# An attention stage issued from a table of work pieces, with queries scaled ahead of their turn

## The chip, the cores and the metric

The kernel runs on one core of a Trainium2 chip. The core has a matrix engine (PE, whose weight loads are listed apart as PEld), three engines for elementwise work (DVE, ACT, POOL), a queue engine (SP) that issues the DMAs, and two on-chip memories: SBUF, which all engines reach, and PSUM, into which PE writes its results. The metric is the device time of one execution in microseconds (us); lower is better.

## The reference

One layer of a hybrid network is computed for 128 context tokens and 512 latent tokens (640 columns in all), in float32. Cut to what matters here:

```python
u = rms_norm(h, g_pre1) * (1 + scale1) + shift1
q, k, v, b_gate, c_gate, x_in, g_att, g_conv = split(u @ w_in)
q = rms_norm(q.reshape(B, N, 16, 64), q_norm)      # 16 query heads, 4 key heads of 64
k = rms_norm(k.reshape(B, N, 4, 64), k_norm)
# latent tokens: rotary on q and k, keys and values = cached context + own
p = softmax(q @ k.T * 64 ** -0.5)                  # one softmax over 640 keys (context: 128)
A = (p @ v) @ w_att_out
Bm = (b_gate * dwconv3(c_gate * x_in)) @ w_conv_out
m = sigmoid(g_att) * A + sigmoid(g_conv) * Bm
h = h + gate1 * rms_norm(m @ w_o, g_post1)
# then the feed-forward part with w_up, dwconv3, silu, w_down and its own norms
```

The modulation vectors (scale, shift, gate) come from `silu(c) @ w_ada + b_ada`.

## The kernel before

Every matmul with weights or activations is done as three products of a high and a low part: a tensor is copied by ACT into a rounded high part (`hi`) and the rest is formed by a subtraction into a low part (`lo`). `mm3` (lines 161 to 163) issues the three products. Cutting a weight tile of 128 x 1024 in this way is one ACT copy and one subtraction (`cut_hi`, lines 700 and 701; `split`, lines 135 and 136, in the later stages).

The attention stage (from line 514 on) runs over four groups `g`, one for each key head with its four query heads. A group has nine steps. Step 0 is the context's own attention (128 queries, 128 keys, four heads). Steps 1 to 8 (class `Step`, `n` from 0 to 7) each take one tile of 128 latent queries and two of its four heads `h`, against 640 keys. A step consists of:

- scores: 12 matmuls (L603) into two rooms of PSUM (`ps2`, two banks each; there are three such rooms). Queries `QH`, `QL` are raw rotated queries; the factor of their normalisation, `rq`, is not in them yet.
- `exps(h)`: the negative maximum on DVE (L739), that maximum times `rq` on ACT (L741), the exponential on ACT with `scale=rq` and the sum of each row (L742).
- `shares()`: the reciprocal of the sums on DVE (L745) and for each `h` the product of 128 x 640 with it on POOL (L750). The tiles `pr` have two buffers.
- `turned()`: DVE turns both halves in blocks of 32 x 32 into the tile `PT` (L755).

Between the steps stand pieces of other work:

- a query tile: `q_part` (24 matmuls into one of two single PSUM banks `S1`), `q_rotate` (rotary: three products on DVE, L543 and L545, their sum on POOL, L546), `squares` on ACT (L550), `factors` on DVE and POOL (L556 to L558), and later `q_turn`: two transposes on PE (L584) into a single bank, the high part on ACT (L587), the low part on DVE (L590).
- the modulation of the second half (`ada2_mm`, 32 matmuls at L214 from two raw tiles of `w_ada`, and `ada2_keep`, one sum on DVE, L235), sixteen times in all; at the end `ada2_fold`.
- nine cuts of raw weight tiles (units 10 to 18) and, in the last two groups, the two gate columns of 128 (`gate_part`, weights of units 16 and 17).
- the product with the values (class `Values`) for each half of the eight steps: `own` (context, L773) and `part` (L782), into one room `ps2` and both single banks `S1`; then `sums` (ACT copies the odd halves to SBUF, L798 and L799; DVE adds the even ones, L805 and L808), `high` on ACT (L812) and `low` (L816, POOL). `part` is called in two goes of five pairs, or of three and seven.

What sets the order: PE, ACT and DVE (and SP outside) execute in the order in which the program issues to them; this is a hand-written order (`manual_schedule`). POOL's instructions in this stage are placed by the compiler's scheduler. The loop over `i` from 0 to 8 has one fixed pattern for each `i`, with small tables (`turn`, `qt`, `room`, `CUTS`, `BLK`): scores of step `i`; a query's turn; a modulation piece; a part of the values; both `exps`; the low part of the turned query; `turned` of the step before; a query part; the factors of the query before; `sums` and `high` of the values if they are complete; `shares`; `low`; a cut; rotary and squares of the query part. Behind the last group come gate 1 (columns 256 to 640), the fold, `turned` of the last step, the change to the sigmoid table (L978), the last values in three pieces, and their sums.

The raw tiles (weights and `w_ada`) come through a ring of three buffers on SP's queue; the list `ring` holds their order, and `ring_used` asks for the next ones when a piece has been used.

## Time and profile before

| | |
|---|---|
| median of 3 runs | 1163.02 us (1162.43 to 1163.92) |
| profiled execution | 1161.01 us, its span in the profile 1159.2 us |
| mean granted clock of PE | 0.968 |
| busy, share of the span | PE 1105.9 us (95%), DVE 827.6 (71%), ACT 564.6 (49%), POOL 173.2 (15%) |
| first score matmul of step 1 in group 0 | at 77.5 us |
| step 0 of groups 1, 2, 3 | at 126.3, 180.6, 235.1 us |
| step 8 of group 3; first matmul behind the stage | at 278.6 us; at 306.7 us |

Times in the profile are counted from the start of the span. A line such as "L750 POOL TENSOR_TENSOR pr<-pr,sm 128x640" is one line of the program on one engine, with the tile that it writes and those that it reads. Busy time counts an engine as busy while an instruction runs on it; PE's matmuls are pipelined, so that a busy PE need not be at its peak. The granted clock is the share of its full speed that PE was allowed. A view of the waits says for each engine on which instruction it waited and which instruction released it; the chain of work is followed back from the last instruction of the kernel to what released each step.

### The profile page before, as it was taken

Reading aid. Unit: us, or ns where it says so; the run is one execution under the profiler, and the core shown is the slowest. Engines: PE = TensorE matmul, PEld = TensorE weight load, DVE = VectorE, ACT = ScalarE, POOL = GpSimd, SP = SyncE. Lnnn points to the kernel's source line nnn. Section 1 sums busy time; section 2 is a strip of 40 time slices with the busy share of each in tenths; the row PEclk is TensorE's granted clock in tenths of the full one; section 3 lists DMA queues with packets and bytes.
Section 4 is the critical chain, followed back from the end, with each engine's and each line's share of the span. In section 5 each row is a group of like instructions: output and inputs, shape, how many; then the busy total and the mean of one; then the engine's idle time right before and its main releaser. Section 6 shows DMA issues by size and latency. Waiting matters only on the chain.

```text
span 1159.2 us, 21001 instructions
## 1 busy us (share of the span) xinstructions
PE 1105.9 (95%) x8605; PEld 1019.1 (88%) x8605; DVE 827.6 (71%) x1235; ACT 564.6 (49%) x1007; POOL 173.2 (15%) x205
## 2 busy tenths in 40 slices
PE   8988788888899999999999999999999999999997
PEld 6787677777799999999999988999999999998786
DVE  5578777766454788888745447888888888888644
ACT  4366555556233544554542246565454555555431
POOL 2057566665000000000000012000000000002001
PEclk9998897988899999999999999999999999999999
DMA  9665335333022322323332543333332333315632
GB/s 336 200 173 149 104 97 134 92 93 92 23 71 60 104 74 87 96 73 92 91 110 74 180 150 130 108 114 105 112 101 91 96 115 103 114 60 182 222 110 90
DMA packets 188989, 133.47 MB, mean 115 GB/s; under 512 B 16914, under 2 KB 171086, under 8 KB 188878
## 3 DMA queue, kind: packets, MB, share of 16 engines
q1 hardware_dynamic: 188782, 132.11, 37.2%
q8 instruction: 67, 1.10, 0.4%
q14 instruction: 28, 0.23, 0.1%
q10 hardware_dynamic: 112, 0.04, 0.0%
HBM read 120.01 MB, written 12.24 MB: 114 GB/s over the span
## 4 chain that ended last, share of the span: by engine, by line
PE 84%; DVE 6%; ACT 3%; POOL 3%; issue 2%; DMA 1%; DVEq 0%; POOLq 0%; SPq 0%; ACTq 0%
PE b L1029 44%; PE b L161 9%; PE b L163 9%; PE b L162 9%; POOL pr L750 3%; PE s1a L161 2%; PE s1a L162 2%; PE s1a L163 2%; PE s L603 2%; ACT pr L742 1%; DVE Y L1513 1%; DVE PT L755 1%; PE s L161 1%; PE s L163 1%; DVE mx L739 1%
## 5 line engine op out<-in xcount | busy, mean ns | idle before, releaser
L1029 PE MATMUL b<-ZB,whi 128*128 128x322 f32 x1024 | 228.5, 310 | 0.0
L1029 PEld LDWEIGHTS b<-ZB,whi 128*128 128x128 f32 x1024 | 173.8, 189 | 1.6
L1029 PE MATMUL b<-ZB,wlo 128*128 128x322 f32 x512 | 159.4, 311 | 0.0
L1029 PE MATMUL b<-MT,whi 128*128 128x320 f32 x608 | 134.1, 308 | 0.0
L1029 PEld LDWEIGHTS b<-MT,whi 128*128 128x128 f32 x608 | 101.6, 188 | 0.0
L1029 PEld LDWEIGHTS b<-ZB,wlo 128*128 128x128 f32 x512 | 96.2, 188 | 0.0
L750 POOL TENSOR_TENSOR pr<-pr,sm 128x640 f32<-128x640 f32 x64 | 86.7, 1377 | 47.5 <-DVE sm L745 46.7
L1029 PE MATMUL b<-MT,wlo 128*128 128x320 f32 x304 | 93.8, 308 | 0.0
L1513 DVE SCALAR_TENSOR_TENSOR Y<-C,cffn,Y 128x642 f32<-128x642 f32 x88 | 80.9, 921 | 0.9
L1016 ACT ACTIVATE whi<-SUM 128x1024 fp32r<-128x1024 f32 x40 | 42.2, 1055 | 79.6 <-DVE SUM L1483 77.2
L136 DVE TENSOR_TENSOR wlo<-raw,whi 128x1024 fp32r<-128x1024 f32 (+1 forms) x31 | 33.7, 1086 | 52.5 <-ACT whi L135 52.0
L1029 PE MATMUL b<-UH,whi 128*128 128x320 f32 x228 | 70.5, 309 | 0.0
L1029 PE MATMUL b<-UL,whi 128*128 128x320 f32 x228 | 70.4, 309 | 0.0
L1029 PE MATMUL b<-UH,wlo 128*128 128x320 f32 x228 | 70.2, 308 | 0.0
L1020 DVE TENSOR_TENSOR wlo<-raw,whi 128x1024 fp32r<-128x1024 f32 (+1 forms) x51 | 50.4, 1020 | 25.3 <-ACT whi L1016 24.4
L1016 ACT ACTIVATE whi<-WB 128x1024 fp32r<-128x1024 f32 x38 | 40.1, 1055 | 54.8 <-DVE WB L1124 54.8
L1037 ACT ACTIVATE p<-b 128x322 f32<-128x322 f32 (+1 forms) x78 | 34.3, 440 | 58.2 <-PE b L1029 58.2
L603 PE MATMUL s<-KH,Q 64*128 64x320 f32 x256 | 44.5, 343 | 18.2 <-ACT pr L742 17.6
L742 ACT ACTIVATE pr<-s,mr,rq 128x640 f32<-128x640 f32 x64 | 56.7, 885 | 4.1 <-ACT mr L741 0.4
L1029 PEld LDWEIGHTS b<-MT,wlo 128*128 128x128 f32 x304 | 57.0, 188 | 0.0
L1040 DVE TENSOR_TENSOR C<-b,p 128x322 f32<-128x322 f32 x40 | 19.7, 492 | 52.3 <-PE b L1029 51.8
L603 PEld LDWEIGHTS s<-KH,Q 64*128 64x128 f32 x256 | 29.8, 191 | 29.5 <-ACT pr L742 24.3
(382 smaller groups left out, 3166.3 us busy)
## 6 DMA issues: line engine op xcount, KB each, us to landing
raw<-in_w_in_dram SPq DMA_DIRECT2D x48, 512.0 KB, 3.5
RAW<-in_w_up_dram SPq DMA_DIRECT2D x40, 512.0 KB, 5.4
raw<-in_w_ada_dram SPq DMA_DIRECT2D x32, 512.0 KB, 4.8
raw<-in_w_down_dram SPq DMA_DIRECT2D x22, 512.0 KB, 4.0
actd<-Y SPq DMA_DIRECT2D x18, 321.0 KB, 2.8
AFB<-actd SPq DMA_DIRECT2D x18, 321.0 KB, 4.5
XT<-in_w_ada_dram SPq DMA_DIRECT2D x9, 512.0 KB, 5.8
raw<-in_w_conv_out_dram SPq DMA_DIRECT2D x9, 512.0 KB, 3.7
```

What stands on the lines that cost most here:

```text
L136: eng.tensor_tensor(out=lo[:, :n], in0=raw, in1=hi[:, :n].bitcast(F32), op=ALU.subtract)
L161: PE.matmul(out, ah, bh, start=start, stop=False)
L162: PE.matmul(out, ah, bl, start=False, stop=False)
L163: PE.matmul(out, al, bh, start=False, stop=stop)
L603: PE.matmul(outs[h], q[rows, pi, :], kk[rows, g, ks], start=n == 0, stop=n == 2, tile_position=(64 * h, 0))
L742: S.activation(self.pr[:, h, :], self.sc[h], AF.Exp, bias=low, scale=rs, accum_out=self.sm[:, h:h + 1])
L750: G.tensor_tensor(out=self.pr[:, h, :], in0=self.pr[:, h, :], in1=self.sm[:, h:h + 1].broadcast_to((128, NTOK)), op=ALU.mult)
L1016: S.activation(to[0], raw, AF.Copy)
L1020: V.tensor_tensor(out=lo, in0=raw, in1=hi.bitcast(F32), op=ALU.subtract)
L1029: PE.matmul(out, p[:, ws], q[:, k, :], start=start and k == 0 and n == 0, stop=stop and k == 3 and n == 2, skip_group_check=True)
L1037: S.activation(t, pair[j][b], AF.Copy)
L1513: V.scalar_tensor_tensor(out=y, in0=crows(j)[i][:, d:d + NACT], scalar=cffn[:, 44 * d + o:44 * d + o + 1], in1=y, op0=ALU.mult, op1=ALU.add)
```

## The change

A table `PLAN` of four texts, one for each group, takes the place of the loop's fixed pattern. Each word is one piece of work; the pieces are issued to all engines in the order of the words. The letters: S scores, x exponentials of one half, r reciprocal, m shares of one half (on POOL with P, on ACT with A), t turn of the shares; Q query part (numbers from 5 on are the next group's tiles), R the rotary products, p their sum (POOL, or DVE with V), q squares, F factors, T query turn, l its low part; A modulation matmuls, K their sum; c a cut (low part on POOL with P, on DVE with V); V values, u one of three ACT copies, a one of three sums, H high, L and M low; G, g, J gate parts; f fold; w the warm-up of the sigmoid; v a load of values. The letters a and b choose a single bank.

What the pieces do differently:

- POOL's instructions of this stage are issued in the written order too.
- Queries are multiplied by their factors `rq` on POOL (`q_scale`, 128 x 256) before they are turned, from tile 3 of group 0 on. The exponential then has no scale, and the small ACT product of the maximum is gone for these tiles; the context's maximum needs no product in groups 1 to 3.
- Of the shares, some halves are done by ACT (a copy with a scale), the others by POOL.
- The low part of a cut is done on POOL or DVE, as the table says.
- The values of a half are one piece of ten pairs instead of two pieces; copies, sums, high and low are pieces of their own, and the sums over the room of two banks are two instructions instead of four.
- Modulation matmuls always go to the last 128 columns of a single bank instead of a room `ps2` at times; queries' buffers `qf` are three instead of two.
- The gate columns are computed in blocks of 320 columns (before 256, 256 and 128, and 256 and 384), gate 1 whole at the end in eight pieces. The warm-up of the sigmoid stands in step 2 of group 3.
- The ring of raw tiles follows the order of A and c in the table. The same loads are made.

```diff
--- before
+++ after
+PLAN = (
+    """
+    cV
+    S1 R3 Q4a cP x00 x10 r0 q3 x11 q4 R4 m00 p3P t0
+    S2 Q5b r1 m11A x20 m10P p4P x21 F3 t1 Aa R5 r2 F4 K
+    S3 q5 m20A m21A T3b x30 Q6a x31 p5V q6 F5 l3 t2 T4b R6 r3
+    S4 l4 m31A m30P x40 x41 p6P t3 Q7a R7 r4 q7 m40P
+    S5 m41A T5b x50 x51 Aa l5 K cP t4
+    S6 r5 m51A F6 x60 m50A V0 x61 p7P t5 u00
+    S7 F7 u10 u20 a00 r6 x71 Q9a x70 a20 a10 m61A r7 m60P q9 R9 t6 T7b H0
+    S8 l7 p9P m71A m70A Aa x80 F9 K x81 t7 Q8b r8 m81P T6a R8 q8 m80A p8P l6 L0P
+    """,
+    """
+    S0 T4b x00 Aa t9 K l4
+    S1 x10 r0 x11 r1 m00 F3 m10P t0 V1 cV u01 u11
+    S2 u21 a01 a11 T3a x21 m11P x20 Q5b a21 t1 R5 r2 q5 l3 m20A p5P
+    S3 m21P x30 Q6b F5 x31 q6 t2 r3
+    S4 H1 Aa R6 m30A x41 m31P p6P Q7b L1P x40 F6 t3 K T5a
+    S5 q7 r4 R7 l5 m40P m41A T6b x50 Aa x51 K p7P l6 cP t4
+    S6 r5 V0 m50A m51A x60 x61 t5 r6 u00 m61P F7
+    S7 u10 u20 a00 m60P a10 x71 Q9a x70 a20 Ab t6 H0 r7 m71A R9 q9
+    S8 m70A K x80 L0P p9P F9 x81 Q8b t7 r8 m81P R8 q8 p8P T7a m80A l7
+    """,
+    """
+    S0 T4b x00 t9
+    S1 x10 x11 Aa K l4 r0 r1 m00 F3 t0
+    S2 cP m11A V1 m10A x20 x21 u11 t1 r2 a11
+    S3 u01 u21 m20P m21P a01 cP T3b x30 a21 Q5a v x31 t2
+    S4 q5 R5 Q6a l3 r3 m30A x40 p5P x41 m31P Ab F5 q6 t3 r4 R6
+    S5 p6P H1 L1P m41A m40A K F6 T5b x50 x51 t4 l5 Q7a q7
+    S6 R7 T6b r5 m51P Aa x61 l6 p7P m50A K F7 x60 r6 V0 t5 m61P u10 u00
+    S7 a10 Ab u20 m60P a00 x70 x71 a20 H0 Q8a q8 t6 r7
+    S8 K m71A m70P R8 Q9b x81 x80 t7 p8P R9 T7a r8 q9 L0P l7 m81P p9P F9 m80A
+    """,
+    """
+    S0 x00 t9
+    S1 Ab x10 r0 x11 m00 G1a K T4b g1 F3 l4 r1 t0 m10P
+    S2 m11P x20 x21 t1 V1 w
+    S3 r2 u01 a01 u21 Aa u11 x30 m21A a21 m20P x31 a11 t2 r3
+    S4 G0b m30A x40 m31P x41 t3 r4 g0
+    S5 m41A K T3a m40P x50 Ab x51 l3 K t4 r5 H1
+    S6 x61 m51P V0 L1V m50P x60 cP r6 u00 u20 t5 m60A a00
+    S7 x70 m61P Aa a20 u10 x71 t6 r7 m70A
+    S8 x80 J0 x81 J1 m71P K t7 r8 m81P J2 cP fa J3 m80A t8 J4 J5 J6 a10 V2 J7 u12 u02 u22 a12 a02 H0 L0V a22 H2 M2
+    """,
+)
...
+        def rotate_sum(t, out, tm, eng=G):
+            if t:
+                eng.tensor_tensor(out=out, in0=out, in1=tm, op=ALU.add)
...
-        def q_rotate(pz, g, t, eng=G):
-            tm = at.tile([128, 4, HD], F32, tag="z", name=nm("zt"), bufs=ZB)
-            qf = qfs[g, t] = at.tile([128, 4, HD], F32, tag="qf", name=nm("qf"), bufs=2)
-            rotate(pz, t, 0, qf, tm, eng)
+        def q_mults(pz, g, t):
+            tm = at.tile([128, 4, HD], F32, tag="z", name=nm("zt"), bufs=ZB) if t else None
+            qf = qfs[g, t] = at.tile([128, 4, HD], F32, tag="qf", name=nm("qf"), bufs=3)
+            rotate_mults(pz, t, 0, qf, tm)
+            return lambda eng=G: rotate_sum(t, qf, tm, eng)
+
+        def q_rotate(pz, g, t):
+            q_mults(pz, g, t)(V)
+
+        def q_scale(g, t, eng=G):
+            eng.tensor_tensor(out=qfs[g, t], in0=qfs[g, t], in1=rq[g][:, t, :].unsqueeze(2).broadcast_to((128, 4, HD)), op=ALU.mult)
...
-        def cut_hi(i):
+        def cut_hi(i, eng):
-            V.tensor_tensor(out=lo, in0=raw, in1=hi.bitcast(F32), op=ALU.subtract)
+            eng.tensor_tensor(out=lo, in0=raw, in1=hi.bitcast(F32), op=ALU.subtract)
...
-                mx, low = small("mx", 1, 2), small("mr", 1, 2)
+                mx, rs = small("mx", 1, 2), 1.0
                 V.tensor_reduce(out=mx, in_=self.sc[h], axis=AX.X, op=ALU.max, negate=True)
-                rs = rq[self.g][:, self.t, 2 * self.pi + h:2 * self.pi + h + 1]
-                S.activation(low, mx, AF.Copy, scale=rs)
-                S.activation(self.pr[:, h, :], self.sc[h], AF.Exp, bias=low, scale=rs, accum_out=self.sm[:, h:h + 1])
-
-            def shares(self):
+                if not self.g and self.t < 3:
+                    low, rs = small("mr", 1, 2), rq[0][:, self.t, 2 * self.pi + h:2 * self.pi + h + 1]
+                    S.activation(low, mx, AF.Copy, scale=rs)
+                    mx = low
+                S.activation(self.pr[:, h, :], self.sc[h], AF.Exp, bias=mx, scale=rs, accum_out=self.sm[:, h:h + 1])
+
+            def inverse(self):
                 V.reciprocal(self.sm, self.sm)
+
+            def shares(self, h, way):
                 if self.ctx:
                     G.tensor_tensor(out=self.pr, in0=self.pr, in1=self.sm.unsqueeze(2).broadcast_to((128, 4, 128)), op=ALU.mult)
-                    return
-                for h in range(2):
+                elif way == "A":
+                    S.activation(self.pr[:, h, :], self.pr[:, h, :], AF.Copy, scale=self.sm[:, h:h + 1])
+                else:
                     G.tensor_tensor(out=self.pr[:, h, :], in0=self.pr[:, h, :], in1=self.sm[:, h:h + 1].broadcast_to((128, NTOK)), op=ALU.mult)
...
-                    for k in range(2):
-                        x, y = (z.rearrange(two, h=2, k=2, b=32)[:, h, :, k] for z in (both[0:64], odd[:, 0:2]))
-                        V.tensor_tensor(out=dst[rows, 0:2, :, k].rearrange("p e q b -> p q e b"), in0=x, in1=y, op=ALU.add)
+                    else:
+                        x, y = (z.rearrange("p e (q k h b) -> p h q k e b", h=2, k=2, b=32)[:, h] for z in (both[0:64], odd[:, 0:2]))
+                        V.tensor_tensor(out=dst[rows, 0:2].rearrange("p e q k b -> p q k e b"), in0=x, in1=y, op=ALU.add)
 
             def high(self):
...
+            for x in PLAN[g].split():
+                kind, n, way = x[0], [int(d) for d in x[1:] if d.isdigit()], x[-1] if x[-1] in "abAPV" and len(x) > 1 else ""
+                bank = S1[way == "b"] if way in ("a", "b") else S1[kind in "TAf"]
+                at_q = (g + n[0] // NT, n[0] % NT) if n else None
+                if kind == "S":
+                    steps[g, n[0]] = Step(g, n[0] - 1 if n[0] else None)
+                elif kind == "x":
+                    steps[g, n[0]].exps(n[1])
+                elif kind == "r":
+                    steps[g, n[0]].inverse()
+                elif kind == "m":
+                    steps[g, n[0]].shares(n[1] if n[0] else 0, way or "PA"[n[1]])
+                elif kind == "t":
+                    steps.pop((g, n[0]) if n[0] < 9 else (g - 1, 8)).turned()
+                elif kind == "Q":
+                    pzs[at_q] = bank[:, 0:256]
+                    q_part(pzs[at_q], *at_q, range(KT))
+                elif kind == "R":
+                    sums[at_q] = q_mults(pzs[at_q], *at_q)
+                elif kind == "p":
+                    sums.pop(at_q)(V if way == "V" else G)
+                elif kind == "q":
+                    sqs[at_q] = squares(pzs[at_q])
+                elif kind == "F":
+                    factors(sqs.pop(at_q), rq[at_q[0]][:, at_q[1], :])
+                    q_scale(*at_q)
+                elif kind == "T":
+                    lows[at_q] = q_turn(*at_q, bank)
+                elif kind == "l":
+                    lows.pop(at_q)()
+                elif kind == "A":
+                    room = bank[:, 384:512]
+                    ada2_mm(n_ada, room)
+                    ring_used(2)
+                elif kind == "K":
+                    ada2_keep(n_ada, room, acc)
+                elif kind == "c":
+                    n_cut += 1
+                    cut_hi(n_cut, V if way == "V" else G)
+                elif kind == "V":
+                    v = values[n[0]] = Values(g - (n[0] == 1), min(n[0], 1))
+                    if not n[0]:
+                        v.own()
+                    v.part(range(10))
+                elif kind == "u":
+                    values[n[1]].copies(n[0])
+                elif kind == "a":
+                    values[n[1]].adds(n[0])
+                elif kind == "H":
+                    values[n[0]].high()
+                elif kind == "L":
+                    values.pop(n[0]).low(V if way == "V" else G)
+                elif kind == "M":
+                    values.pop(n[0]).low(V)
+                elif kind == "v":
+                    for i in (2, 3):
+                        v_group(i)
+                elif kind == "G":
+                    pzs["G", n[0]] = bank[:, 0:NTOK // 2]
+                    gate_part(pzs["G", n[0]], 16, n[0], range(KT))
+                elif kind == "g":
+                    S.activation(gate0[:, slice(*BLKS[n[0]])], pzs["G", n[0]], AF.Copy)
+                elif kind == "J":
+                    if gate1 is None:
+                        gate1 = ps2()[:, OFF:OFF + NTOK]
+                    b, k = n[0] // 4, n[0] % 4
+                    gate_part(gate1[:, slice(*BLKS[b])], 17, b, range(2 * k, 2 * k + 2))
+                elif kind == "f":
+                    ada2_fold(acc, bank)
+                elif kind == "w":
+                    S.activation(warm, mhalf[:, 0:1], AF.Sigmoid)
```

181 lines of the change are left out of this document (50 added, 131 removed).

## The prediction

> **What bounds the kernel now.** I read the page first: its chain of work is mostly matmuls of the later stages, and its 40 slices show the dips of PE and of its clock in the attention stage. Then the view of windows, cut at the first score matmul of each group (columns: length, then busy time of PE, PEld, DVE, ACT and POOL with instruction counts, granted clock, DMA share, GB/s): groups 0 to 3, the tail from step 8 of group 3 on, and the rest of the kernel:
>
> ```profile
> 77.47:126.28 48.81, 39.23 (x514) 33.73 (x514) 39.00 (x73) 29.70 (x72) 33.47 (x33) 0.86 0.41 113
> 126.28:180.59 54.31, 46.37 (x719) 39.35 (x718) 42.07 (x81) 30.89 (x76) 34.62 (x35) 0.87 0.48 123
> 180.59:235.12 54.53, 46.30 (x719) 39.28 (x718) 41.84 (x81) 30.90 (x76) 34.48 (x34) 0.87 0.33 98
> 235.12:278.60 43.48, 38.81 (x679) 32.58 (x678) 31.75 (x55) 24.18 (x62) 23.89 (x21) 0.92 0.40 116
> 278.60:306.71 28.11, 20.48 (x224) 17.06 (x225) 10.55 (x30) 8.85 (x19) 6.67 (x5) 0.75 0.04 12
> 330.00:1159.20 829.20, 820.21 (x5032) 777.13 (x5030) 599.92 (x780) 394.20 (x612) 23.00 (x44) 1.00 0.34 108
> ```
>
> In the last row PE is full at clock 1.00, so what the attention stage gains or loses passes to the end. In the stage no engine is full: in group 2 DVE works 41.84 of 54.53 us, and PE is granted 0.87 of its clock. A mean of 0.87 over 54.5 us is 14 us at half clock. The same view in three slices of 3.41 us shows one place:
>
> ```profile
> 169.89:173.30 3.41, 1.55 (x12) 1.07 (x12) 2.06 (x5) 2.94 (x8) 0.18 (x1) 1.00 0.44 127
> 173.30:176.72 3.42, 1.50 (x7) 1.53 (x8) 3.38 (x10) 1.56 (x4) 1.69 (x2) 0.50 1.18 213
> 176.72:180.13 3.41, 3.41 (x18) 3.41 (x17) 1.71 (x3) 1.99 (x5) 3.41 (x3) 0.50 1.15 169
> ```
>
> A slice in which PE works 1.55 us is followed by two at clock 0.50. This place costs 1.86 + 1.92 us of idle, then half of 1.50 and of 3.41 us: 6.2 us. The clock column counts such places: two slices are 6.8 us, so groups 0, 1 and 2 with 14 us each have two, group 3 has one (0.08 x 43.5 x 2 = 7 us), the tail two. Two places are 12.4 us of a group.
>
> Why PE stands still is told by the chain of work, here at that place (start, length, what):
>
> ```profile
> 165.65 3.46 POOL pr L750 x2
> ...
> 170.32 0.98 ACT pr L742 x2
> 171.32 0.87 ACT PT L798 x2
> ...
> 175.22 0.66 PE s1b L584 x2
> ```
>
> Both shares of a step stand on POOL (3.46 us), the exponentials follow, and behind them in ACT's queue the copies of the values, then DVE's sums (left out here, to 175.2); only then are the two single banks free for the turn of the next queries (L584). A serial chain of ten us (165.65 to 175.22) runs through four queues in which every step is issued in one fixed order.
>
> **The change part by part.** Durations, from the groups of the window of group 2, by engine (count | busy us, mean ns | idle before, releaser):
>
> ```profile
> L739 DVE TENSOR_REDUCE mx<-s 128x1 f32<-128x640 f32 x16 | 12.4, 816 | 1.3 <-PE s L603 1.2
> L755 DVE STREAM_TRANSPOSE PT<-pr 128x1280 f32<-128x1280 f32 x8 | 12.0, 1503 | 1.7 <-POOL pr L750 1.7
> L701 DVE TENSOR_TENSOR wlo<-raw,whi 128x1024 fp32r<-128x1024 f32 x2 | 3.9, 1926 | 1.3 <-ACT whi L700 1.3
> ...
> L808 DVE TENSOR_TENSOR PT<-s,PT 64x192 f32<-64x192 f32 x4 | 1.2, 342 | 0.3 <-ACT PT L799 0.3
> ```
> ```profile
> L741 ACT ACTIVATE mr<-mx,rq 128x1 f32<-128x1 f32 x16 | 4.6, 288 | 6.8 <-DVE mx L739 6.6
> ```
> ```profile
> L750 POOL TENSOR_TENSOR pr<-pr,sm 128x640 f32<-128x640 f32 x17 | 22.9, 1371 | 10.7 <-DVE sm L745 10.5
> L558 POOL TENSOR_TENSOR rq<-ssq,mhalf 128x4 f32<-128x4 f32 x5 | 5.1, 1017 | 0.1
> L546 POOL TENSOR_TENSOR qf<-qf,zt 128x256 f32<-128x256 f32 x4 | 2.9, 735 | 0.0
> L816 POOL TENSOR_TENSOR AL<-PT,AH 128x768 fp32r<-128x768 f32 x1 | 1.8, 1846 | 0.0
> L816 POOL TENSOR_TENSOR AL<-PT,AH 128x512 fp32r<-128x512 f32 x1 | 1.3, 1292 | 0.0
> ```
>
> *DVE, group 2.* Both cuts (L701, 2 x 1.93) go to POOL; the sums of L808, eight in a group, become four of twice the elements (at most 4 x 0.34 = 1.4 saved, at least nothing, as the elements stay; I take 0.6, since 192 elements at one a ns would leave 0.15 of each); the context's product of four numbers goes (within 0.2, counted). 41.8 - 3.9 - 0.6 - 0.2 = 37.1 us. Group 1 keeps one cut: 39.4.
>
> *ACT.* Scaling the queries beforehand removes the 16 small L741 (4.6 us), in group 0 only for tiles 3 and 4. Eight of 16 shares move here. The trace has no such copy; the nearest are L742, 0.98 from PSUM with its sum (170.32), and a 640-wide sigmoid from SBUF:
>
> ```profile
> 308.46 0.74 ACT L994 ACTIVATE MA<-gate 128x640 f32<-128x640 f32 x1 [0.81 <-DVE AL L816]
> ```
>
> Eight are 5.9 to 7.8 us; I take 0.8 each, as source and target are like L994: 30.9 - 4.6 + 6.4 = 32.7.
>
> *POOL.* Eight shares remain, 1.37 each in the mean and 1.73 in the pair at 165.65: 11 to 13.8 us. The new scaling of 256 elements is at most L546's 0.74, five times, and as L546 adds two whole tensors hardly less; a cut of 1024 goes by the two L816 rows (0.55 for 256 more) on to 2.4, twice: 34.5 - 22.9 + 11 + 3.7 + 4.8 = 31, or 34 with slow shares. Each now stands in a written order: behind a cut wait the next share and the factors (L558, 1.0) of the next query.
>
> *PE* does the same work. Its need at full clock, by rows of undisturbed steps:
>
> ```profile
> 155.83 0.41 PE L603 MATMUL s<-KH,Q 64*128 64x320 f32 x2
> ...
> 157.29 0.39 PE L161 MATMUL s1a<-whi,UH 128*128 128x256 f32 x1
> ...
> 160.13 0.28 PE L163 MATMUL s1a<-whi,UL 128*128 128x256 f32 x1
> ...
> 161.42 1.08 PE L214 MATMUL s1b<-raw,s 128*32 128x128 f32 x32
> ...
> 300.42 0.39 PE L782 MATMUL s<-PT,KL 32*64 32x256 f32 x4
> 300.64 0.39 PE L782 MATMUL s<-PT,KL 32*64 32x256 f32 x4
> ```
>
> Scores and a turn take 1.46 (155.83 to 157.29), about 1.0 and 0.45; a query part ends 160.13 + 0.1, 2.9; modulation 1.05; values 20 rounds of 0.22 and the context's own 0.4, 4.8 for a half. A group: 8 x 1.0 + 0.6 + 5 x 2.9 + 4 x 1.05 + 2 x 4.8 + 5 x 0.45 = 39 us. With DVE at 37 to 39 these are the floors, against 54.5 now.
>
> *What goes and what is late next.* I walked the rows of group 2 by hand in queue order. Where values end, PE goes on with scores, and the turn waits only for one copy and one pair of sums (0.5 + 0.7 us) instead of the whole chain; a query part then hides the other copies. What is late next is step 2's scores: they wait for step 1's first exponential, which stands behind DVE's transposes, the rotation, the low part and the context maximum left from step 8 and step 0; PE idles some 2.6 us there. Elsewhere waits of 0.2 to 0.8 us remain at the banks. By the slices above a 2.6 us gap may halve the clock once more, 1.7 to 3.4 us. So of 12.4 us a group I take 8.5 as gained (46 us a group, DVE at 0.83 of it against 0.77 now). Bounds: 4 and 14.
>
> The Trainium skill ("TensorE: Matmul & The Clock Gate", Part 1, HAM oscillation) puts the limit at idle gaps above some 3.4 us. By that rule the 2.6 us gap would cost no clock and the sum would be about 6 us lower over three groups; the rows speak against it, since two idle stretches with work between them halved the clock at a slice 45% busy.
>
> *Group 0* has three of five query tiles in the old form and starts against the last key work; of two places I take the later one and a little: -7 (bounds -3 and -13). *Group 3* has one place, fewer queries and one cut moved: -5.5 (bounds -2 and -10).
>
> *The warm-up for the sigmoid* moves from behind the last exponential to step 2 of group 3, with 12 exponentials still to come. Now one table load stands between the last exponential and the first sigmoid:
>
> ```profile
> 288.44 1.28 ACT L978 ACT_TABLE_LOAD   x1
> ```
>
> If each change of function reloads, there are three loads in place of one; the first lies beside the values, the second delays step 3's exponential, the third lies beside PE's next stage: +1.3 us (bounds 0 and 2.6).
>
> The Trainium skill ("ScalarE: Activation LUTs", Table sets: the hidden batching unit) lists exp and sigmoid in different sets and advises to group calls by set; by it the three loads are certain; were the page wrong, the sum would be 1.3 us lower. No row here shows an exponential behind a sigmoid.
>
> *Tail.* Now 28.1 us from step 8's scores to the first matmul of the next stage, because gate parts, the fold and a shares-transpose stand ahead of the last values on PE, at half clock; then ACT waits:
>
> ```profile
> ACT PT L798 <- PE s1b L782: 14.5, 1, 14.5
> ```
>
> After it the order is scores 1.1, two maxima 1.6, exponential and its sum 1.1, reciprocal 0.15, share 1.25, transpose 1.5, values 4.8, copies 1.3, sums 1.5, and the other half's high and low 1.8 put between, with ten handovers of 0.1: 17 us; gate 1 (eight pieces of 0.9) fills PE beside it. I take -10.5 (bounds -6 and -12).
>
> *DMA.* The same loads stand on SP's queue in another order, and the DMA share is 0.33 to 0.48 in the groups: taken as 0. Two modulation pieces of group 1 are one step apart, so a load may end a step late once; the bound is that step's 4.5 us.
>
> **Sum.** -7 - 8.5 - 8.5 - 5.5 - 10.5 + 1.3 = -38.7 us. The profiled execution took 1161.0 (span 1159.2), so 1122.3; the median of the three runs is 2.0 above it: **1124**. The rest shifts with it.
>
> **The rivals.** (a) *The clock stays halved.* Values as one piece of 4.8 us hold both single banks longer than the two parts did. If the turn behind them comes late by 1.9 us in a slice, only the idle part of each place is won, 3.1 of 6.2: seven places give 22, the tail 6, minus 1.3: -27, 1136, and up to 1146 if the tail keeps its second gap. For: the bank wait exists now (175.22). Against: scores lie between. (b) *DVE-bound packing.* All places go and groups end near 40 to 41 us: -11 - 14 - 14 - 8 - 12 + 1 = -58, 1105. For: my walk's floor is near it. Against: two engines at 0.95 at once. (c) *Nothing:* the order is a list, but DVE's strict queue sets the same waits, 1163 within 0.2%. Against: the two places have named causes that the list takes apart. (d) *Slower: POOL's queue.* A query now passes factors (1.0 us), scaling 0.7, and may stand behind a cut of 2.4 and a share, before its turn; PE waits in order at the turn, with the next scores and query part behind it, and DVE waits for those. Seventeen queries take this way; from 2.3 us late each the 39 us are gone; with a cut and a scaling ahead of each, 3.1 x 17 = 53, it is 1177. Against: only seven of the nine cuts are POOL's, and it is at 31 to 34 of 46 us.
>
> **How the numbers follow.** Forecast 0.62 (own range 1112 to 1136), (a) 0.20, (b) 0.10, (c) 0.03, (d) 0.05. A measurement of this kernel tells 0.2%, 2.3 us, from no change. Faster 0.92, same 0.03, slower 0.05. The range 1107 to 1146 takes in the forecast, nearly all of (a) and a part of (b).
>
> **What would show it.** Group windows of 45 to 47 us with DVE at 37 to 39, a granted clock of 0.92 or more; the wait of POOL's shares for reciprocals (10.5 us in a group) mostly gone; the small L741 gone in groups 1 to 3; three table loads; the tail at 17 to 18 us. Group windows at 50 with clock 0.87 would show (a); PE waiting at the turn for POOL would show (d). The prediction is wrong if the gaps merely move.

## The result, and the profile after

| | before | changed |
|---|---|---|
| median of the runs | 1162.72 us (1160.84 to 1163.92) | 1116.2 us (1113.74 to 1117.22) |
| profiled execution | 1161.0 us, span 1159.2 | 1117.1 us, span 1115.3 |
| granted clock, mean | 0.968 | 0.993 |

The ratio is 0.9598, its interval 0.9576 to 0.962. The time of 1116.2 us lies in the range, 8 us below the forecast of 1124.

The view of windows for the changed kernel, cut as before: groups 0 to 3, the tail from step 8 of group 3 on, the rest. Columns: length, then busy time of PE, PEld, DVE, ACT and POOL (instructions in brackets), granted clock, DMA share, GB/s.

```profile
77.80:121.38 43.58, 39.57 (x540) 34.34 (x539) 35.34 (x71) 32.82 (x75) 27.21 (x32) 0.96 0.43 120
121.38:165.08 43.70, 40.96 (x719) 35.20 (x718) 38.49 (x78) 30.15 (x68) 30.23 (x32) 1.00 0.44 131
165.08:208.61 43.53, 40.86 (x719) 35.18 (x719) 36.77 (x72) 30.23 (x68) 28.47 (x29) 1.00 0.62 149
208.61:244.05 35.44, 32.61 (x630) 27.23 (x629) 28.40 (x52) 25.02 (x56) 19.11 (x19) 0.95 0.31 91
244.05:263.32 19.27, 15.97 (x224) 13.30 (x225) 12.22 (x22) 7.18 (x14) 5.26 (x4) 0.91 0.38 111
286.00:1115.30 829.30, 820.36 (x5033) 777.27 (x5031) 599.92 (x780) 394.32 (x612) 22.72 (x44) 1.00 0.35 108
```

The stage went from 229.2 us (77.47 to 306.71) to 185.5 (77.80 to 263.32); what lies behind it kept its length (852.5 and 852.0). Group by group: -5.2, -10.6, -11.0, -8.1 us, the tail -8.8, in sum -43.7. Two kinds of loss went. The clock column gives 62 us at half clock in the stage before (13.7 + 13.7 + 13.7 + 6.8 + 14.0) and 10 now (one slice of 3.4 in group 0, in group 3 and in the tail). A slice at half clock loses half of the time in which PE works in it, and before the change PE stood still for a part of many of them, so the 52 us are worth less than 26. The PE column tells the parts: over the five windows PE is busy 191.2 us before and 170.0 after, for nearly the same matmuls (2855 and 2832 records), and idle 38.0 and 15.5 us. So some 21 us of the gain are clock, and some 22 are idle time that went.

The groups of instructions in the window of group 2 (count | busy us, mean ns | idle before, releaser), the rows that answer the prediction's durations:

```profile
L809 ACT ACTIVATE pr<-s,mx 128x640 f32<-128x640 f32 x16 | 12.6, 790 | 4.3 <-DVE mx L804 4.1
L825 DVE STREAM_TRANSPOSE PT<-pr 128x1280 f32<-128x1280 f32 x8 | 12.0, 1500 | 0.0
L820 POOL TENSOR_TENSOR pr<-pr,sm 128x640 f32<-128x640 f32 x8 | 9.9, 1254 | 9.4 <-DVE sm L812 9.4
L818 ACT ACTIVATE pr<-pr,sm 128x640 f32<-128x640 f32 x8 | 6.4, 824 | 1.3 <-DVE sm L812 1.3
L760 POOL TENSOR_TENSOR wlo<-raw,whi 128x1024 fp32r<-128x1024 f32 x2 | 4.8, 2390 | 0.0
L637 POOL TENSOR_TENSOR qf<-qf,rq 128x256 f32<-128x256 f32 x4 | 2.5, 613 | 0.3
```

A share on ACT is 0.82 us, on POOL 1.25; DVE's transposes no longer wait for a share (0.0 idle before them, 1.7 before). POOL still waits 9.4 us for reciprocals, now for eight shares (10.7 us for seventeen before), though the prediction expected this wait to go mostly. It is idle time of POOL: over the whole stage the transposes wait for one of its shares once, 0.8 us.

The view of waits (engine, line, releaser: us, times, longest) of the stage, PE's two largest before and then after:

```profile
PE s L603 <- ACT pr L742: 17.6, 16, 4.0
PE s1b L584 <- DVE tabk L235: 12.7, 6, 2.7
```
```profile
PE s L661 <- ACT pr L809: 4.4, 7, 1.2
PE s L852 <- DVE PT L825: 2.0, 1, 2.0
```

The scores' wait for exponentials fell from 17.6 to 4.4 us, the queries' turn has left the top of the list, and 2.0 us stand at one place in the tail.

### The profile page after: what moved, and what is told of

The parts are those of the page before. It is cut to its first block, busy times and chain, and to the rows that moved or that the text cites. A ratio compares the mean times of both kernels' runs of the same rounds, so it can differ in the third digit from the quotient of the medians.

```text
span 1115.3 us, 20886 instructions
## 1 busy us (share of the span) xinstructions
PE 1082.4 (97%) x8581; PEld 999.5 (90%) x8581; DVE 815.6 (73%) x1211; ACT 567.5 (51%) x983; POOL 149.8 (13%) x194
## 4 chain that ended last, share of the span: by engine, by line
PE 82%; DVE 7%; ACT 2%; issue 1%; POOL 0%; DVEq 0%; POOLq 0%; ACTq 0%
PE b L1079 46%; PE b L209 9%; PE b L207 9%; PE b L208 9%; PE s L852 2%; PE s L661 2%; DVE mx L804 1%; DVE PT L825 1%; DVE Y L1563 1%; PE s1b L852 1%; ACT pr L809 1%; PE s1a L207 1%; DVE PT L882 0%; PE s1b L207 0%; PE s1a L208 0%
## 5 line engine op out<-in xcount | busy, mean ns | idle before, releaser
L1079 PE MATMUL b<-UH,whi 128*128 128x320 f32 x228 | 70.5, 309 | 0.0
L1070 DVE TENSOR_TENSOR wlo<-WB,whi 128x1024 fp32r<-128x1024 f32 x38 | 46.5, 1223 | 8.9 <-ACT whi L1066 8.9
L1066 ACT ACTIVATE whi<-raw 128x1024 fp32r<-128x1024 f32 (+1 forms) x51 | 43.5, 892 | 18.2 <-PE b L209 9.8
L804 DVE TENSOR_REDUCE mx<-s 128x1 f32<-128x640 f32 x64 | 50.2, 811 | 3.3 <-PE s L661 3.0
L809 ACT ACTIVATE pr<-s,mx 128x640 f32<-128x640 f32 x56 | 44.1, 791 | 15.7 <-DVE mx L804 13.2
```

The costliest lines, as they stand in the source:

```text
L804: V.tensor_reduce(out=mx, in_=self.sc[h], axis=AX.X, op=ALU.max, negate=True)
L809: S.activation(self.pr[:, h, :], self.sc[h], AF.Exp, bias=mx, scale=rs, accum_out=self.sm[:, h:h + 1])
L1066: S.activation(to[0], raw, AF.Copy)
L1070: V.tensor_tensor(out=lo, in0=raw, in1=hi.bitcast(F32), op=ALU.subtract)
L1079: PE.matmul(out, p[:, ws], q[:, k, :], start=start and k == 0 and n == 0, stop=stop and k == 3 and n == 2, skip_group_check=True)
```

## The experiments

The times as ratio to the kernel before, with the stage's length in each profile, the part of it that is the tail (from step 8 of group 3 on), and the stage's time at half clock (from the clock column in slices of 3.41 us). Each ratio is to runs of the kernel before from the same session (medians of 1159.8 to 1162.7 us), so it is not the quotient of the medians listed. Differences in per cent are differences of these ratios; 1% is 11.6 us.

| run | ratio, interval | median us | stage us | of it the tail us | half clock us |
|---|---|---|---|---|---|
| before | 1 | 1162.7 | 229.2 | 28.1 | 62 |
| changed kernel | 0.9598, 0.9576 to 0.962 | 1116.2 | 185.5 | 19.3 | 10 |
| e3: new order, shares, cuts and scaling as before | 0.9891, 0.9874 to 0.9908 | 1149.5 | 218.0 | 19.1 | 38 |
| e5: only shares as before | 0.9893, 0.9864 to 0.9922 | 1148.6 | 217.0 | 22.8 | 38 |
| e6: only scaling as before | 0.969, 0.9664 to 0.9716 | 1124.9 | 193.4 | 19.6 | 14 |
| e7: only cuts as before | 0.9725, 0.9706 to 0.9743 | 1128.9 | 195.8 | 17.3 | 20 |
| e8: only values in two goes | 0.9801, 0.9781 to 0.9821 | 1137.7 | 203.7 | 17.6 | 14 |
| e4: old order, values in two goes | 0.9817, 0.9796 to 0.9837 | 1141.9 | 211.0 | 18.1 | 41 |
| e11: old order, values whole | 0.9982, 0.997 to 0.9993 | 1160.0 | 230.4 | 19.1 | 61 |
| e1: warm-up late | 0.9584, 0.9569 to 0.96 | 1114.9 | 184.3 | 19.0 | 7 |
| e2: last cut late | 0.9587, 0.957 to 0.9603 | 1115.2 | 182.0 | 15.8 | 7 |
| e12: both | 0.9561, 0.9547 to 0.9576 | 1111.5 | 179.4 | 15.6 | 3 |
| e10: both, and a start | 0.9563, 0.9549 to 0.9577 | 1111.3 | 180.7 | 15.6 | 3 |
| e13: both, and another start | 0.9563, 0.955 to 0.9576 | 1110.7 | 179.6 | 15.6 | 3 |

The prediction credits the order with the cleared places. The rival is that the new division of the work (shares on two engines, cuts on POOL, scaled queries) does it in any order. The first two kernels below take one away each.

**e3: the new order with the old division.** In the table every `m..A` becomes `m..P`, every `cP` becomes `cV`, and the exponential takes its scale again:

```diff
-                    q_scale(*at_q)
...
-                if not self.g and self.t < 3:
-                    low, rs = small("mr", 1, 2), rq[0][:, self.t, 2 * self.pi + h:2 * self.pi + h + 1]
+                if True:
+                    low, rs = small("mr", 1, 2), rq[self.g][:, self.t, 2 * self.pi + h:2 * self.pi + h + 1]
```

> The new order with the old division of work: all shares on POOL, low parts of all cuts on DVE, queries not scaled, so that each exponential has its small ACT product and its scale again. Theory O (the order holds the gain): no engine's load passes 41 us of a group's 43.6, so groups of 44 to 48 us and 1120 to 1133 us. Theory D (the gain is the load taken off POOL, DVE and ACT): the chain of two shares is back, groups of 50 to 54 us with half-clock slices, 1142 to 1162 us.

Measured: 1149.5 us. The order, with the values whole, keeps 1.1 of the 4.0%, and nearly all of it is the tail: the tail is 9.0 us shorter than before (28.1 to 19.1), the four groups together only some 2 us (201.1 to 199.0). The half clock is back (38 us).

**e4: the old fixed order, written as a table, with the new division,** values in two goes as before. Two of group 0's three cuts keep their low part on DVE. The tail is like the new one, but it has the warm-up behind the last exponential, and neither a cut nor sums of the first half in it:

```diff
+    S1 Ab V1 x10 x11 t0 F4 r1 m10P m11A cP
+    S2 W1 x20 x21 t1 u11 u01 u21 a11 a01 a21 H1 r2 m20P m21A K L1P
+    S3 T3b x30 x31 l3 t2 Q5a r3 m30P m31A R5 p5P q5
```

> The old fixed order of steps 0 to 7 in all four groups, written as a table (values in two goes, sums behind the exponentials in one block, modulation and cuts at their old places), with the new division of work (one share on POOL and one on ACT, scaled queries, cuts on POOL); the tail from step 8 of group 3 is the new one, with the warm-up behind the last exponential. Theory O: the blocks behind the exponentials bring back both gaps in each group, groups of 49 to 53 us with clock 0.87 to 0.93, 1140 to 1155 us. Theory D: groups of 44 to 47 us, 1115 to 1130 us.

Measured: 1141.9 us, 1.8 of the 4.0%, of which the tail is 10.0 us in the profile (28.1 to 18.1); the four groups are 8.3 us shorter (201.1 to 192.8), against 34.9 in the changed kernel (166.3). So neither explains the gain: alone they bring 1.1 and 1.8%, and more of that in the tail than in the groups; together (with whole values) they bring 4.0%. Some changes are kept in both kernels and were not tried alone: POOL's written order, the third buffer of the queries, the sums in fewer instructions, the gate blocks of 320 columns. The next four undo one part each in the changed kernel.

**e5: all shares on POOL,** nothing else:

```diff
-    S3 q5 m20A m21A T3b x30 Q6a x31 p5V q6 F5 l3 t2 T4b R6 r3
+    S3 q5 m20P m21P T3b x30 Q6a x31 p5V q6 F5 l3 t2 T4b R6 r3
```

> The changed kernel with all shares on POOL again (eight more a group, 1.25 us each, in the same places of the order). Theory "POOL's queue decides": POOL goes from 28 to 38 busy us of a 43.5 us group, the second share of a step ends 1.25 us later, the transposes with it; groups of 47 to 50 us with half-clock slices back, 1133 to 1142 us (most of the 33 us that the old division costs in the new order). Rival "POOL has room": groups stay within 1 us, 1115 to 1121.

Measured: 1148.6 us, 2.95% above the changed kernel and as slow as e3, where all three parts are undone. Its groups are 49.6, 46.6, 55.9 and 42.0 us (in the changed kernel 43.6, 43.7, 43.5 and 35.4). The window of group 2, the longest, then the waits over the stage:

```profile
173.78:229.72 55.94, 47.35 (x719) 39.04 (x718) 36.68 (x72) 24.58 (x60) 39.52 (x42) 0.85 0.46 116
```
```profile
DVE PT L825 <- POOL pr L820: 35.0, 22, 4.7
ACT pr L809 <- DVE mx L804: 34.4, 26, 3.2
...
PE s1b L642 <- POOL qf L637: 5.6, 4, 2.0
```

DVE waits 35.0 us with its transposes for POOL's second share (in the changed kernel 0.8, in one wait); the next maxima stand behind the waiting transpose in DVE's queue, so the exponentials wait 34.4 us for them (13.2 there); and PE waits 5.6 us at the queries' turn for the scaling, which stands behind shares on POOL: the prediction's rival (d) in small. The theory of POOL's queue held; the time lies some 7 us past its upper end. A wait of the transposes is 1.6 us in the mean, more than the 1.25 of one share; POOL's queue also holds cuts and scaling here, and in e3, where it holds neither, the transposes wait 17.6 us. That DVE and POOL hold each other up (last section) is not what costs here: in group 2 a share on POOL takes 1.25 us and DVE is busy 36.7 us, as in the changed kernel (1.25 and 36.8).

**e6: queries unscaled,** the second part of e3's edit alone.

> The changed kernel with queries turned unscaled in all groups: the 16 small ScalarE products of a group are back (0.29 us each, 4.6 us), the exponential takes its scale from a column (0.79 becomes 0.885), and the eight POOL scalings of 0.6 us a group go. Theory "ACT has room" (30 of 43.5 us busy): each step's first exponential comes 0.3 to 0.4 us later, 9 steps, 3 us a group at most and mostly hidden: 1117 to 1125 us. Rival "the products stand on the path": full 4.6 + 1.5 us a group, with a slice of half clock more in some, 1135 to 1145.

Measured: 1124.9 us, 0.9% above the changed kernel, at the end of what the theory of room allowed. The small products are 4.6 us a group again, and the exponential with its scale from a column takes 885 ns where the changed kernel's takes 790 (row L809 above):

```profile
L808 ACT ACTIVATE pr<-s,mr,rq 128x640 f32<-128x640 f32 x17 | 15.0, 885 | 0.9
L806 ACT ACTIVATE mr<-mx,rq 128x1 f32<-128x1 f32 x16 | 4.6, 287 | 3.1 <-DVE mx L803 3.1
```

Group 2 is 3.0 us longer (46.5), for 5.0 us more of busy ACT (35.2 against 30.2).

**e7: all lows of the cuts on DVE** (`cP` becomes `cV`, seven in all).

> The changed kernel with all lows of the cuts on VectorE (1.93 us each, seven more in all; POOL loses 2.4 each). Theory "VectorE's work bounds the groups" (36.8 to 38.5 of 43.5 us busy now): two cuts in groups 0 and 2, one in group 1, one in group 3 and one in the tail add up to 13 us: 1121 to 1130 us. Rival "VectorE has slack": within 3 us of the change, 1114 to 1119; the tail may gain 2 us, as POOL's long cut then does not stand beside the modulation sums.

Measured: 1128.9 us, 1.3% or 15 us above the changed kernel. The time lies in the theory's span, but not by its sum. The cut takes 1.2 us here, not 1.93:

```profile
L760 DVE TENSOR_TENSOR wlo<-raw,whi 128x1024 fp32r<-128x1024 f32 x2 | 2.4, 1204 | 0.5 <-ACT whi L759 0.5
```

So do six of the seven; the tail's takes 2.14, beside a share on POOL. Together that is 9.4 us, and the stage has ten further us at half clock (20 against 10). In the profile the four groups are 12.3 us longer, and the tail is 2.0 us shorter, as the expectation supposed: the fold's products take 0.17 to 0.18 us there.

**e8: values of a half in two goes,** in the new order; the second go (`W`) behind the next step's scores, copies and sums behind it:

```diff
-    S6 r5 V0 m50A m51A x60 x61 t5 r6 u00 m61P F7
-    S7 u10 u20 a00 m60P a10 x71 Q9a x70 a20 Ab t6 H0 r7 m71A R9 q9
+    S6 r5 V0 m50A m51A x60 x61 t5 r6 m61P F7
+    S7 W0 u00 u10 u20 a00 m60P a10 x71 Q9a x70 a20 Ab t6 H0 r7 m71A R9 q9
```

> The changed kernel with the values of a half in two goes (the first three or five pairs, then the rest behind the next step's scores or maxima, with the copies and sums behind that). Theory "the gain is order and division, not the whole step": 1114 to 1121 us. Rival "whole values free the single banks early": the next query part waits for the second go as it did before, 2 to 4 us at seven places, some with a slice of half clock: 1130 to 1145.

Measured: 1137.7 us, 2.0% above: the rival held. Its waits over the stage:

```profile
ACT PT L872 <- PE s1b L852: 37.6, 8, 9.4
DVE PT L882 <- ACT PT L872: 31.8, 8, 6.2
PE s L661 <- ACT pr L809: 9.9, 16, 1.5
```

In the changed kernel the three are 18.9, 13.6 and 4.4. The copies and sums wait at the head of ACT's and DVE's queues for the second go, and with them the maxima and exponentials behind. Most of it is idle time of PE (29.0 us of the stage against 15.5; the half clock is 14 us against 10). By the view of its waits PE stands 10.5 us until a copy or a sum has freed a single bank (1.7 in the changed kernel), at no place more than 1.5 us, so the rival's 2 to 4 us at a place were too much. A likely reason, not shown, is that the second go comes on top of a step that has a query part already. Another placing might cost less; that was not tried.

**e11: the old order with whole values,** e4 with the words `W` taken out.

> The kernel of the old order with the new division, this time with the values of a half whole in one step (everything else as in that run, 1141.9 us). Theory "whole values gain only with copies, sums and scores placed for them": without the new order the step's copies and sums stay where they were, the 4.8 us piece holds PE ahead of the next scores, and the time is 1136 to 1146 us. Rival "whole values gain by themselves, some 20 us in either order" (as splitting them in the new order cost 22): 1118 to 1126.

Measured: 1160.0 us, 18 us slower than e4 and further than the theory went. By the ratios, values in one piece gain 2.0% (24 us; 18 in the profiled stage) in the new order and lose 1.65% (19 us, and 19 in the stage) in the old. The two edits are alike but not the same: in e8 some copies and sums moved behind the second go as well. Waits over the stage, of e4 and then of e11:

```profile
DVE mx L803 <- PE s L660: 16.3, 18, 3.4
...
PE s L660 <- ACT pr L808: 5.9, 2, 4.1
```
```profile
DVE mx L803 <- PE s L660: 39.0, 21, 5.1
ACT pr L808 <- DVE mx L803: 22.6, 13, 4.2
PE s L660 <- ACT pr L808: 21.0, 14, 4.1
```

DVE's maxima wait 39.0 us for scores in place of 16.3. Why is seen in the windows of the step with values (from its scores to the next) and of what follows it, in group 1: first e11, where two steps follow, then the changed kernel, one step.

```profile
166.22:174.84 8.62, 7.45 (x237) 6.35 (x236) 4.29 (x9) 4.65 (x8) 7.01 (x10) 1.00 0.42 124
174.84:187.96 13.12, 9.46 (x58) 8.26 (x52) 9.18 (x16) 7.55 (x15) 6.40 (x4) 0.61 0.75 142
```
```profile
147.69:154.50 6.81, 6.62 (x208) 5.18 (x204) 5.74 (x10) 5.36 (x11) 3.41 (x2) 1.00 0.63 185
154.50:160.11 5.61, 5.22 (x77) 4.65 (x69) 4.80 (x9) 4.05 (x8) 3.25 (x5) 1.00 0.21 63
```

In e11 DVE has 4.29 us of work in the 8.62 us of the step with values, scores and modulation; then the old order has nothing for PE but scores, where the second go stood, PE waits for the exponentials and the clock falls to 0.61. The changed kernel puts a query part and modulation into the step behind the values (5.22 of 5.61 us busy) and leaves DVE 5.74 us of work beside them. So whole values don't gain by themselves; they gain in an order made for them. Whether the matmuls behind them or the scattered copies and sums count for more was not tried.

**e1: the warm-up behind the last exponential again; e2: the last cut behind the last turn.**

```diff
-    S2 m11P x20 x21 t1 V1 w
+    S2 m11P x20 x21 t1 V1
...
-    S8 x80 J0 x81 J1 m71P K t7 r8 m81P J2 cP fa J3 m80A t8 J4 J5 J6 a10 V2 J7
+    S8 x80 J0 x81 J1 m71P K t7 r8 m81P J2 cP fa J3 m80A w t8 J4 J5 J6 a10 V2 J7
```
```diff
-    S8 x80 J0 x81 J1 m71P K t7 r8 m81P J2 cP fa J3 m80A t8 J4 J5 J6 a10 V2 J7
+    S8 x80 J0 x81 J1 m71P K t7 r8 m81P J2 fa J3 m80A t8 J4 J5 J6 cP a10 V2 J7
```

> The warm-up of the sigmoid goes back behind the last exponential (group 3, step 8); nothing else changes. Theory (the two table loads at 219.4 and 222.99 us stand on the path of step 3's exponentials and the half-clock slice from 225.2 us follows from them): one table load fewer pair in the stage, group 3 shorter by 1.3 to 3 us, 1113 to 1115 us. Rival (the loads lie beside the values and step 3 waits for DVE's sums anyway): group 3 stays at 35.4 us and the time at 1116.

> The last cut moves from ahead of the fold to behind the last turn of shares; nothing else changes. Theory (two of the fold's small DVE products, 1.03 and 2.14 us in the changed kernel, are held up by POOL's share and by its 2.4 us cut, the last turn starts 2 us late behind them, PE stands 2 us and the last values run at half clock): the long product shrinks to 0.2 us, the last turn starts near 251.2 instead of 253.2 us, the tail is 15 to 16 us instead of 19.3, the time 1112 to 1113. Rival (the turn waits for ACT's or POOL's share anyway): tail 19, 1116.

Measured: 1114.9 and 1115.2 us; each interval overlaps the changed kernel's, so alone neither is a gain that the medians tell. The profiles show the places: with the late warm-up group 3 is 32.7 us in place of 35.4, and with the late cut the tail is 15.8 in place of 19.3. In e1's profile a slice at half clock stands in group 2, where the changed kernel has none, and takes 1.6 us back. e2's profile is of the slowest of its runs: there the stage begins 2.4 us later (80.25 against 77.80), behind 10 us at half clock in the earlier stages that the changed kernel's profile does not have.

**e12: both.**

> The changed kernel with the sigmoid's table behind the last exponential again and the last half's cut behind the last turn. By the two single runs: group 3 loses 2.7 us (35.4 to 32.7), the tail 3.5 (19.3 to 15.8), together 1111 to 1113 us. Rival "the clock's slices take it back": each alone gained only 1.3 to 2 us in the median, so the two together give 1112 to 1115 with single runs from 1108 on.

Measured: 1111.5 us, its runs from 1109.68 to 1111.79, all below the lowest of the changed kernel (1113.74); the intervals of the ratios meet at 0.9576, so that a gain of some 0.4% is at the edge of what the runs tell. Windows of group 3 and of the tail in its profile:

```profile
208.25:241.13 32.88, 31.14 (x629) 25.81 (x628) 28.39 (x52) 22.25 (x53) 19.29 (x19) 1.00 0.34 98
241.13:256.75 15.62, 14.28 (x225) 12.22 (x225) 10.25 (x22) 8.79 (x16) 5.12 (x4) 1.00 0.48 136
```

Both stand at full clock: 2.6 and 3.7 us less than in the changed kernel.

**e10 and e13: two other starts of group 0,** on top of e12. One slice at half clock is left there. In the changed kernel ACT stands 2.5 us with a cut, and the first exponentials stand behind it:

```profile
80.62 1.06 ACT L759 ACTIVATE whi<-raw 128x1024 fp32r<-128x1024 f32 x1 [2.54 <-PE s1a L209]
```

The expectation of e10 takes this for the wait for a load. The row names PE instead, and the cut's load, issued at 70.5 us, had landed by 74.2: the cut writes one of three buffers of high parts, and PE's query part (to 81.7 us) still reads high parts.

```diff
-    S1 R3 Q4a cP x00 x10 r0 q3 x11 q4 R4 m00 p3P t0
+    S1 R3 Q4a x00 x10 cV r0 q3 x11 q4 R4 m00 p3P t0
```
```diff
-    S1 R3 Q4a cP x00 x10 r0 q3 x11 q4 R4 m00 p3P t0
+    S1 R3 Q4a x00 x10 r0 q3 x11 cV q4 R4 m00 p3P t0
```

> As the run with both edits of group 3 and the tail, and at the start of the stage the cut for tile 4 behind the first two score columns, its low on VectorE: the first maxima no longer wait behind ScalarE's high of the cut, which itself waited 2.54 us for a load. Theory "the load's wait stands on the start's path": group 0 loses 1.5 to 2.5 us against that run, 1108 to 1112. Rival "VectorE's queue takes it over" (1.9 us more on VectorE, and the query part later): within 1 us of that run, or up to 2 us slower.

> As the run with both edits of group 3 and the tail (1111.49 us), and at the start of the stage the cut for tile 4 behind step 1's second exponential, its low on VectorE behind the second maximum: neither the maxima and exponentials nor the reciprocals stand behind it, as the reciprocal did in the last start. Theory "the start's half-clock slice comes from the cut ahead of the exponentials" (slice 34% busy, gaps of 1.49 and 0.78 us): the gaps close, the slice at half clock goes, group 0 loses 2 to 4 us (43.6 to 40 to 41.6): 1107.5 to 1109.5. Rival "the start is short of work anyway" (few scores, queries still to come): the gap moves to the query's turn in step 2, within 1 us of 1111.5.

Measured: 1111.3 and 1110.7 us, both within 1 us of e12. The time of e10 lies in its theory's span too, but group 0 is 45.1 and 44.0 us, against 43.6 with the start as it was: the rivals held. The gap closes and others open: in e13 PE waits 0.8 us at a query's turn for the scaling, 0.8 for the cut's low part and 1.0 at later scores, and half clock follows there, 7 us later than in e12. One of these waits:

```profile
89.42 0.41 PE L661 MATMUL s<-KH,Q 64*128 64x320 f32 x1 [0.63 <-ACT pr L809]
```

## Why the prediction was right, point by point

**The bound was read rightly:** idle places of PE, each with slices at half clock, and the rest of the kernel shifting with the stage. 52 of 62 us at half clock went.

**Groups 1 and 2** (-8.5 forecast, -10.6 and -11.0 measured). The term was too small by 2 to 2.5 us each, because it kept one idle place with half clock. The gap ahead of step 2's scores was put at 2.6 us; it measured 1.18, as the view of the timeline shows for PE in group 2:

```profile
170.78 0.41 PE L661 MATMUL s<-KH,Q 64*128 64x320 f32 x1 [1.18 <-ACT pr L809]
```

Its slice is 62% busy and no half clock followed (rows in the last section). The group is 43.5 us, 4.5 above PE's forecast floor of 39. DVE's work was forecast well: 36.77 (37.1 forecast) and 38.49 (39.4). ACT has 30.2 in place of 32.7: the exponential's gain from a fixed scale, 16 x 0.095 = 1.5 us, was not foreseen. POOL has 28.5 in place of 31: shares at 1.25 and scaling at 0.61.

**What was credited with it** is the step that fell short. The prediction has the list of pieces take the two places apart and costs the division as busy time of engines that are not full. By e3 the list with the old division keeps 13 us, 9 of them in the tail and some 2 in the four groups, for which the forecast had 29.5. In e5, without ACT's shares, the transposes stand 35.0 us for POOL, though POOL is no more than 39.5 of 55.9 us busy in the longest group. The division was worth its place in the chain (two shares side by side, 0.82 and 1.25 us, instead of one behind the other, 2.5, and behind POOL's cuts and scaling), not the busy time that it moved. And the values as one piece, which the prediction names only as a risk (rival a) and gives no gain, bring 24 us in this order.

**The total** is near in part by luck. In the profiles the terms make -43.7 us where -38.7 was forecast, and the misses have both signs: groups 1, 2 and 3 gained 2.1, 2.5 and 3.8 us more than forecast, group 0 and the tail 1.8 and 1.7 less.

**Group 0** (-7, measured -5.2) lies in its bounds; the slice at half clock at the start stays, and neither of the two edits tried (e10 and e13) removes the half clock.

**Group 3 and the warm-up** (-5.5 + 1.3, measured -8.1). Without the warm-up in it, group 3 is 32.9 us (e12): -10.6, past the bound of -10, again for the missing half clock; the window also has 50 matmuls fewer than before (679 and 629). The early warm-up costs 2.6 us, the upper bound, not 1.3. The timeline of ACT shows two loads in group 3:

```profile
219.41 1.28 ACT L1035 ACT_TABLE_LOAD   x1
222.99 1.28 ACT L809 ACT_TABLE_LOAD   x1 [0.81 <-DVE mx L804]
```

A third stands at the next stage's first sigmoid. So the three loads of the prediction are in the trace. The Trainium skill ("ScalarE: Activation LUTs", Table sets: the hidden batching unit), which the prediction cites there, lists exp and sigmoid in different sets; the trace agrees. The second load thins out the slice from 221.83 (49% busy), and the next runs at half clock: as an estimate 1.28 + 3.41 / 2 = 3.0 us, of which 2.6 reach the end.

**The tail** (-10.5, measured -8.8; 19.3 us, not 17 to 18). The walk left out one thing: DVE held up by POOL. Timelines of DVE and of POOL in the changed kernel (start, length):

```profile
249.87 1.03 DVE L292 TENSOR_TENSOR mod<-mod,feat 128x16 f32<-128x16 f32 x1
...
251.10 2.14 DVE L292 TENSOR_TENSOR mod<-mod,feat 128x16 f32<-128x16 f32 x1
```
```profile
249.61 1.25 POOL L820 TENSOR_TENSOR pr<-pr,sm 128x640 f32<-128x640 f32 x1 [1.86 <-DVE mod L289]
250.83 2.37 POOL L760 TENSOR_TENSOR wlo<-raw,whi 128x1024 fp32r<-128x1024 f32 x1
```

A product of 128 x 16 (L292, both inputs in SBUF) on DVE takes 2.14 us and ends with POOL's cut (251.10 + 2.14 = 253.24; 250.83 + 2.37 = 253.20); without a neighbour it takes 0.17 (e2's timeline, below). The last transposes stand behind it, PE idles 2.0 us (L852 above), and half clock takes 1.7 more. With the cut moved the tail is 15.8 and 15.6 us, so -12.3 and -12.5, slightly past the bound of -12. The walk's 17 us are then more than 1 us too long, so that two misses partly cancel in the forecast.

**DMA** at nothing: right, by the unchanged rest; the share in group 2 rose to 0.62, and the group is no longer than group 1 with 0.44.

**Rivals.** (a) did not come: the work placed beside and behind the whole values covers them (e11 is the case without). (b) at 1105 is still below the best run (1109.1). (d) hardly shows in the changed kernel, where PE waits at a turn for POOL once, 0.4 us. It shows where parts are undone, as waits at a turn for the scaling: 5.6 us in e5, and 5.7 and 6.2 us in e4 and e11, where the old order has half of the shares on ACT all the same.

## What to carry to other kernels

A piece of work should be moved off an engine for its place in a serial chain first: half of the shares on ACT were worth 34 us in this order, though POOL without that had 39.5 us of work in 55.9. Busy totals tell little about it. Joining two pieces into one and reordering are one decision: a like joining gained 24 us in the order made for it and lost 19 in the old one. New order and new division gave some 2 and 8 us in the four groups alone, and 35 together. Nor do the parts of the division add up (34, 11 and 15 us when undone singly, 34 when undone together), so a version is judged whole.

## What was not expected of the hardware

**DVE and POOL stop each other.** Timelines of e2, first DVE, then POOL:

```profile
252.01 0.17 DVE L292 TENSOR_TENSOR mod<-mod,feat 128x16 f32<-128x16 f32 x1
...
252.30 1.03 DVE L292 TENSOR_TENSOR mod<-mod,feat 128x16 f32<-128x16 f32 x1
...
253.53 0.17 DVE L292 TENSOR_TENSOR mod<-mod,feat 128x16 f32<-128x16 f32 x1
253.63 1.50 DVE L825 STREAM_TRANSPOSE PT<-pr 128x1280 f32<-128x1280 f32 x1
```
```profile
252.05 1.25 POOL L820 TENSOR_TENSOR pr<-pr,sm 128x640 f32<-128x640 f32 x1 [1.86 <-DVE mod L289]
253.80 2.38 POOL L760 TENSOR_TENSOR wlo<-raw,whi 128x1024 fp32r<-128x1024 f32 x1 [0.50 <-ACT whi L759]
```

The product with both inputs in SBUF takes 0.17 us when it starts ahead of the share (252.01) or between the share and the cut (253.53), and ends with the share (253.3) when it starts behind it. The transpose, with one input, and the cut run side by side and keep their 1.50 and 2.38 us. It goes both ways, as the kernel before shows, POOL and then DVE:

```profile
190.87 3.45 POOL L750 TENSOR_TENSOR pr<-pr,sm 128x640 f32<-128x640 f32 x2
```
```profile
191.42 1.78 DVE L701 TENSOR_TENSOR wlo<-raw,whi 128x1024 fp32r<-128x1024 f32 x1 [0.79 <-ACT whi L700]
```

Two shares take 3.45 us, not 2 x 1.25, and the cut 1.78, not the 1.2 of e7. The durations of 1.93 and 1.73 that the prediction took for work were partly this. The Trainium skill ("SBUF — State Buffer", Terms, shared port pair) says that the two share a pair of ports, held for a whole instruction while the other is blocked; the rows agree.

**The clock follows what PE did in the slice before.** Slices of 3.41 us of the changed kernel, two at a time:

```profile
167.22:170.63 3.41, 2.11 (x43) 1.42 (x39) 3.41 (x6) 2.60 (x13) 0.00 (x0) 1.00 1.36 202
170.63:174.04 3.41, 3.26 (x91) 2.80 (x99) 2.74 (x8) 3.41 (x8) 2.65 (x4) 1.00 1.08 249
221.83:225.24 3.41, 1.68 (x39) 1.04 (x35) 3.09 (x7) 2.59 (x6) 0.27 (x1) 1.00 0.28 76
225.24:228.65 3.41, 3.41 (x17) 3.08 (x18) 2.66 (x4) 2.49 (x5) 0.95 (x1) 0.50 0.78 236
```

A slice 62% busy leaves the clock, one 49% busy halves the next. Over all fourteen kernels, between 77 and 262 us, of the slices that themselves ran at full clock all 45 with PE under half busy were followed by half clock, 9 of 37 between 0.5 and 0.7, and none of 586 above 0.7. (At half clock the same matmuls keep PE busy longer; there 8 of 60 slices above 0.7 were followed by another at half clock.) What counts is the idle time of the slice as a whole: at the start of the changed kernel two gaps of 1.49 and 0.78 us in one slice, 33% busy, were enough. In every run the clock changes only at whole multiples of 3.41 us from its first change, so the grid stands still while the work shifts over it; that can decide whether a gap costs 1.7 us more. The runs of one kernel, 1113.74 to 1117.22 us, follow their mean clocks of 0.996 to 0.991; in which slices they differ was not recorded.
